# A hybrid decoder trunk on one core: half words joined after five weight units instead of two, and one block of queries turned by TensorE

## The chip, the cores and the metric

The kernel runs on 1 core of one Trainium2 chip. The metric is the device time of one execution in microseconds. A core has TensorE (PE in the profile; PEld is its weight load), VectorE (DVE), ScalarE (ACT), GpSimd (POOL) and SyncE (SP), and 16 DMA engines that all issuing queues share.

## The reference

Two post-norm layers on 256 tokens of width 2048. Each layer has a mixer of two head groups and a SwiGLU block:

```
def _hybrid_mixer(x, positions, w_in, ...):
    qa, ka, va, qi, wi, ki, cq, ckv, kr = split(x @ w_in)
    qa, ka = _rope(qa, rot 32), _rope(ka, rot 32)            # group A: 8 heads of 128
    qi, ki = _rope(qi, rot 16), _rope(ki, rot 16)            # indexer: 16 heads of 64
    score = sum over heads of relu(qi . ki) * wi, causal     # picks the top 64 keys of a query
    out_a = softmax(qa . ka over the picked keys) @ va
    q_b = _rms_norm(cq, g_cq) @ w_uq                         # group B (MLA): 8 heads
    q_nope, q_pe = q_b[..., :128], _rope(q_b[..., 128:], rot 64)
    kv = _rms_norm(ckv, g_ckv) @ w_ukv                       # k_nope, v_b
    out_b = causal softmax of (q_nope . k_nope + q_pe . _rope(kr)) @ v_b
    return concat(out_a, out_b) @ w_o

x = _layer_norm(ALPHA * x + mixer(x));  x = _layer_norm(ALPHA * x + swiglu(x))
```

All inputs and outputs are float32.

## The kernel before

**Weight units.** All tokens stay on the chip and the weights stream past them. A weight unit is 2 x 128 rows by 512 columns: one 512 KB load (`raw`) from SyncE's queue, split into two parts of reduced precision, `wh` by ACT (L427) and `wl` by DVE (L428), and then twelve matmuls on TensorE (two token tiles, two row blocks, three products: L391 to L393). There are five buffers of `wh` and of `wl` in this stage (`UNITS`), and four of `raw`. A projection chunk of 512 columns (`in_chunk`, `dsa_qk`, `dsa_v`) is 8 units.

**Tasks and ticks.** What has to be done with a projection's result (rope, turning, attention) is written as Python generators. `spawn` starts one; `tick()` stands after each weight unit and counts `units_gone`; a generator that yields `n` goes on `n` units later; `behind(...)` yields one unit at a time until other tasks are done, and `finish(...)` runs tasks out. So the position of a step in the program is counted in weight units.

**Order.** The program order that results is a priority. When the program is built, the tile framework sets each engine's own order: among the instructions that it reckons ready it takes the earliest in program order, so one whose operands or buffers it reckons not ready is passed by later ones (`tc.high_priority` raises a few by hand). On the chip each engine then runs its list strictly in order and waits where an operand is late.

**The attention stage of a layer** in program order, with its weight units: QI0 (8 units, first half of the indexer queries), TA (8), QI1 (8, second half), TB (8, the low-rank inputs `cq`, `ckv`), KA0 (8, four heads' keys of group A), then 2 units for the rope part of the MLA queries (`w_uq[2]`), `mla_half(0)` (4 ticks: queries `qn` twice, keys `kn`, values `vb`), QA0 (8), VA0 (8), `mla_half(1)`, KA1, QA1, VA1, and the output projection. The tasks:

- `heads_T` (L605 to L630) ropes a projection of 512 columns on DVE (L284 to L288) and turns it, 128x128 by 128x128, so that features stand on partitions. It does so with the DMA: ACT parts each 32-bit word into its half words (`pl`, L619), a transposing DMA that ACT issues turns the half words (L622), and ACT joins them again into `dst` (L627). It is used for QI0, QI1, KA0, QA0, KA1, QA1 and the rope queries: 7 blocks of two token tiles in each layer. Its yields: 1 after the rope, 1 after each token tile's parting and DMA, then 2 more, then a join and 1 for each tile.
- `indexer` (L702) waits behind TA's, QI0's and QI1's tasks, makes the scores in six steps of two units each (matmuls L714, ACT's relu L719, DVE's weighted sum L724) and then picks the top keys on DVE, 8 a unit (L731, L732).
- `mla_attend(hp)` (L773) handles two heads: it waits `wait` units and behind the rope queries' task (for the first two pairs), puts the logits into one PSUM pair of banks that all `att()` users share (L788 for the plain part, L792 for the rope part), and goes through `attend` (L562): DVE reads the logits (L571), softmax on DVE and ACT (L555 to L560), three transposes on TensorE into a bank of `trp()` (L424, two banks in turn), ACT copies (`pr`, L582), and one unit later the product with the values (L589).
- `dsa_attend(hp)` (L812) does the same for group A, behind the indexer and the tasks of its keys and queries.

The other work of this stage that shares the queues: `presums` (L833) loads weight blocks of the SwiGLU from POOL's queue, adds them on DVE (L852 to L856) and stores the sums. The small working tiles `ra`, `rb`, `hd`, `pl`, `lg`, `pr`, `rel` all come out of ten buffers of 2 KB a partition (`t2`).

Of the kernel before, what the change touches and what calls it, by code (L numbers as in the profile page):

```python
# [28 lines left out]
AF = mybir.ActivationFunctionType  # L29
# [4 lines left out]
P = 128  # L34
D = 2048
S = 256
NT = S // P
# [26 lines left out]
BYK = 3  # L64
SOON = 200
FIRSTD = 2
T2, T2MORE = 4, 6
ALLFROM, SETSFROM, EARLY = 3, 4, 0

# [16 lines left out]
def hybrid_trunk(ctx: ExitStack, tc: tile.TileContext, x, xt_in, pos, w_in, g_cq, g_ckv, w_uq,  # L86
                 w_ukv, w_o, ln1_g, ln1_b, ln1_T, w_gu, w_down, ln2_g, ln2_b, ln2_T, out):
    nc = tc.nc
# [11 lines left out]
    def t8(shape, dt, s):  # L100
        return sb.tile(shape, dt, name=nm(s), tag="a8", bufs=10)
# [17 lines left out]
    def t4(shape, dt, s):  # L119
        return pt(shape, dt, s, "a4", 8)  # L120

    def t2(shape, s, dt=F32):
        if phase["name"] == "att":
            phase["t2"] = phase.get("t2", 0) + 1
            if phase["t2"] * T2MORE % (T2 + T2MORE) < T2MORE:
                return pt(shape, dt, s, "t2", T2MORE)
        return sb.tile(shape, dt, name=nm(s), tag="t2", bufs=T2)
# [10 lines left out]
    def in_turn(s, first, n):  # L138
        turns[s] = turns.get(s, -1) + 1
        return bank(first + turns[s] % n, s)  # L140
# [4 lines left out]
    def trp():  # L145
        return in_turn("tr", 4, 2)
# [71 lines left out]
    sinM = const.tile([P, NT, 2, 32], F32, name="sinM")  # L218
# [57 lines left out]
    def rope(dst, src, nh, hd, rot, cos, sin):  # L276

        half = rot // 2
        s3 = src.rearrange("p (h d) -> p h d", d=hd)
        d3 = dst.rearrange("p (h d) -> p h d", d=hd)  # L280
        a = t2([P, nh, 2, half], "ra")
        b = t2([P, nh, 2, half], "rb")
        for j in range(2):
            nc.vector.tensor_tensor(a[:, :, j, :], s3[:, :, j * half:(j + 1) * half],  # L284
                                    cos.unsqueeze(1).to_broadcast([P, nh, half]), op=ALU.mult)
            nc.vector.tensor_tensor(b[:, :, j, :], s3[:, :, (1 - j) * half:(2 - j) * half],
                                    sin[:, j, :].unsqueeze(1).to_broadcast([P, nh, half]), op=ALU.mult)
        nc.vector.tensor_tensor(d3[:, :, 0:rot], a.rearrange("p h j k -> p h (j k)"),  # L288
                                b.rearrange("p h j k -> p h (j k)"), op=ALU.add)
# [19 lines left out]
    def spawn(gen):  # L309
        task = [0, gen]  # L310
        tasks.append(task)
        step(task)
        return task
# [5 lines left out]
    def finish(*ends):  # L319
        while any(e in tasks for e in ends):  # L320
            for task in list(tasks):
                if any(e in tasks for e in ends):
                    step(task)
# [53 lines left out]
    def proj(units, lhs, n, before=None, split_t=None, banks=None):  # L377

        o = [bank(i, "acc") for i in banks] if banks else [acc() for _ in range(NT)]
        loaded = []
        last = len(units) - 1

        def go(t, u):
            (wh, wl), ks = loaded[u], units[u][1]
            for j, k in enumerate(ks):
                h, l = lhs(t, k)
                a, b = wh[:, j, :n], wl[:, j, :n]
                first, final = u == 0 and j == 0, u == last and j == len(ks) - 1  # L390
                mm(o[t][:, :n], h, a, start=first, stop=False)  # L391
                mm(o[t][:, :n], h, b, start=False, stop=False)  # L392
                mm(o[t][:, :n], l, a, start=False, stop=final)  # L393

        def go_by_k(u):

            (wh, wl), ks = loaded[u], units[u][1]
            for j, k in enumerate(ks):
                xs = [lhs(t, k) for t in range(NT)]
                for i, w in ((0, wh), (1, wh), (0, wl)):  # L400
                    for t in range(NT):
                        mm(o[t][:, :n], xs[t][i], w[:, j, :n], start=u == i == j == 0 and w is wh, stop=False)

        for u, (src, ks) in enumerate(units):
            if before is not None:
                before(u)
            early = before is not None and u < BYK
            loaded.append(load_unit(src, src.shape[-1], KU if early else 1))
            if early:
                go_by_k(u)  # L410
            else:
                for t in range(1 if split_t else NT):
                    go(t, u)
            tick()
        if split_t:
            split_t()
            for u in range(len(units)):
                go(1, u)
                tick()
        return o  # L420

    def transpose4(srcs, psum):
        for i, s in enumerate(srcs):
            nc.tensor.transpose(psum[:, i * P:(i + 1) * P], s, ident)  # L424
# [169 lines left out]
    def layer(l, xT, norms, last):  # L594
        xk = xlhs(xT)

        def in_chunk(b, before=None, split_t=None):
            n = IN_BLOCKS[b][1]
            return proj([(w_in[b][l, u], range(u * KU, (u + 1) * KU)) for u in range(NKT // KU)], xk, n,
                        before, split_t)  # L600
# [1 line left out]
        cosI = [cosA[:, t, 0::2] for t in range(NT)]  # L602
        sinI = [sinA[:, t, :, 0::2] for t in range(NT)]

        def heads_T(o, nh, hd, rot, cos, sin, dst):  # L605


            ss = []
            for t in range(NT):
                s = t2([P, C], "hd")  # L610
                if rot < hd:
                    nc.scalar.activation(s, o[t], AF.Copy)
                rope(s, o[t], nh, hd, rot, cos[t], sin[t])
                ss.append(s)
            yield 1
            turned = []
            for s in ss:
                h16 = t2([P, 2 * C], "pl", U16)
                nc.scalar.activation(h16.rearrange("p (h c) -> p h c", h=2),  # L619
                                     s.bitcast(U16).rearrange("p (c h) -> p h c", h=2), AF.Copy)  # L620
                v = s.bitcast(U16).rearrange("p (k t) -> p k t", t=P)
                nc.scalar.dma_start_transpose(v, h16)  # L622
                turned.append(v)
                yield 1
            yield 2
            for t in range(NT):
                nc.scalar.activation(  # L627
                    dst[:, :, t * P:(t + 1) * P].bitcast(U16).rearrange("p k (t h) -> p h k t", h=2),
                    turned[t].rearrange("p (h k) t -> p h k t", h=2), AF.Copy)
                yield 1  # L630
# [131 lines left out]
        def mla_half(hf):  # L762
            qn = t4([P, 4, S], F32, "qn")
            kn = t4([P, 4, S], F32, "kn")
            vb = t4([P, NT, C], F32, "vb")
            nope_T(qn, [w_uq[hf][l, u] for u in range(2)], QL // P, cqT)
            nope_T(kn, [w_ukv[hf][l, 0]], KVL // P, ckvT)
            o = proj([(w_ukv[2 + hf][l, 0], range(2))], ckk, C)
            for t in range(NT):
                nc.scalar.activation(vb[:, t, :], o[t], AF.Copy)  # L770
            return qn, kn, vb
# [100 lines left out]
        if l == 0:  # L872
            turn("att")
            warm_up(18)
            o = in_chunk(QI0, load_xT)
            make_masks()
            rope_tables()
        else:
            o = in_chunk(QI0, None, lambda: finish(*norms))
# [9 lines left out]
        qpT = t4([P, M_HEADS // 2, S], F32, "qpT")  # L889
        bias = [pt([P, P * (t + 1)], F32, f"selb{t}") for t in range(NT)]  # L890
        o = in_chunk(TA)
        aff(1)
        p_ta = spawn(ta_post(o))
        aff(2)
        o = in_chunk(QI1)
        p_qi1 = spawn(heads_T(o, 8, I_DIM, I_ROT, cosI, sinI, qiT[1]))
        aff(3)
        p_ix = spawn(indexer())
        o = in_chunk(TB)
        p_tb = spawn(tb_post(o))  # L900
        if l == 0:
# [3 lines left out]
        finish(p_tb)  # L905
        o = proj([(w_uq[2][l, u], range(u * KU, (u + 1) * KU)) for u in range(QL // P // KU)], cqk, C)
        p_qp = spawn(heads_T(o, M_HEADS, M_ROPE, M_ROPE, [cosM[:, t] for t in range(NT)],
                             [sinM[:, t] for t in range(NT)], qpT))
        m = mla_half(0)
        b = [spawn(mla_attend(0, m, 1, p_qp)), spawn(mla_attend(1, m, 4, p_qp))]  # L910
        qa, p_qa = dsa_qk(QA0)
# [17 lines left out]
        for c in range(D // C):  # L929
            o = proj([(w_o[l, c, k // KU], range(k, k + KU)) for k in first], olhs, C)  # L930
# [271 lines left out]
        def spawn_hidden(fc, g, u):  # L1202
            hT = t8([P, 2, 4, S], F32R, "hT")
            held.append((fc, hT, spawn(hidden(g, u, hT, 3, 2 if fc + 1 < FIRSTD else 4))))

# [4 lines left out]
        def down_half(fc):  # L1210

            down(held[:2], (2, 3) if fc % 2 else (0, 1), ((2, 3), (0, 1)), first_operands if fc == ALLFROM else None)
            if fc % 2:
                del held[:2]
# [13 lines left out]
        for fc in range(1, NFC):  # L1228
            order = ORDER.get(fc, "SSQS")
            if fc >= FIRSTD:  # L1230
                down_half(fc)
                finish_hidden()
            g, u = gate_up(fc, [({"N": "plain", "S": "wino", "Q": "made", "T": "two"}[k], v) for k, v in zip(order, UNIT[order])],
                           finish_hidden if fc < FIRSTD else None)
            if fc < FIRSTD:
                for c in range(2, D // C):
# [18 lines left out]
    for l in range(DEPTH):  # L1255
        xT, norms = layer(l, xT, norms, l == DEPTH - 1)
# [51 lines left out]
```

## Time and profile before

| | us |
|---|---|
| median of 3 runs | 2172.12 |
| lowest, highest run | 2170.91, 2173.5 |
| the profiled execution | 2171.01 |
| its span, first to last instruction | 2169.2 |

The profile shows one execution, on the one core. The granted TensorE clock is 0.996 of full over the span. In the page, a group's line gives the source line, engine and operation, output and inputs by the program's names, the count, busy time and mean duration, and the idle time of its engine just before with what ended it. In a timeline, a line gives start, duration, engine, source line and operation, and in brackets the idle time before it and what released it; ACTq is ACT's queue when it issues a DMA, during which ACT starts nothing else. The attention stage is roughly 0 to 335 us in layer 0 and 1106 to 1420 us in layer 1.

### The profile page before, as it was taken

How to read it: one execution, taken by the hardware profiler on the slowest of the kernel's cores; microseconds unless marked ns; L12 is line 12 of the kernel's file. 1: busy time of each engine (PE TensorE's matmuls, PEld its weight loads, DVE VectorE, ACT ScalarE, POOL GpSimd, SP SyncE). 2: the span in 40 equal slices, each digit the busy share in tenths (PEclk: the TensorE clock that was granted, in tenths of full speed). 3: DMA queues.
4: the chain of work that ended last, by engine and by line, in shares of the span. 5: the costliest groups of instructions: out<-in, count | busy, mean ns of one | idle time of the engine just before them, and what ended most of it. 6: DMA issues, size and time to landing. Idle time of an engine off the chain costs nothing.

```text
span 2169.2 us, 28289 instructions
## 1 busy us (share of the span) xinstructions
PE 2125.2 (98%) x9830; PEld 1757.5 (81%) x9830; DVE 1859.4 (86%) x2359; ACT 1358.0 (63%) x1730; POOL 330.7 (15%) x527
## 2 busy tenths in 40 slices
PE   8999999999999999999999899999999999999998
PEld 7877888888878888888878788888888888888886
DVE  6596776899999999999855977768999999999997
ACT  6565664666666667766655565547666766666673
POOL 1112220021111101110012213200211111101111
PEclk9999999999999999999999999999999999999999
DMA  8878888578988889988678889895888988889884
GB/s 257 267 220 312 284 320 313 189 210 272 252 255 284 276 285 288 278 270 260 213 161 241 274 277 313 296 331 175 214 266 257 267 276 279 284 276 298 271 302 122
DMA packets 192336, 568.69 MB, mean 262 GB/s; under 512 B 47824, under 2 KB 48128, under 8 KB 191552
## 3 DMA queue, kind: packets, MB, share of 16 engines
q1 hardware_dynamic: 110736, 398.38, 51.5%
q0 software_dynamic: 51600, 160.77, 29.1%
q10 hardware_dynamic: 29856, 7.74, 2.6%
q8 instruction: 77, 1.26, 0.2%
q14 instruction: 67, 0.55, 0.1%
HBM read 506.51 MB, written 31.46 MB: 248 GB/s over the span
## 4 chain that ended last, share of the span: by engine, by line
PE 74%; DVE 9%; DMA 7%; issue 6%; ACT 3%; POOL 1%; ACTq 0%; SPq 0%; DVEq 0%; POOLq 0%
PE acc L1175 7%; PE acc L1176 7%; PE acc L1174 7%; PE acc L392 6%; PE gu_p L1060 6%; PE gu_p L1057 6%; PE gu_p L1059 6%; PE acc L393 6%; PE acc L391 6%; DVE wl L428 4%; PE gu_c L1059 3%; PE gu_c L1060 3%; PE gu_c L1057 3%; DMA hd<-pl 2%; DMA raw<-in_w_in_dram 2%
## 5 line engine op out<-in xcount | busy, mean ns | idle before, releaser
L428 DVE TENSOR_TENSOR wl<-raw,wh 128x1024 fp32r<-128x1024 f32 (+2 forms) x925 | 1088.2, 1211 | 206.6 <-ACT wh L427 203.9
L427 ACT ACTIVATE wh<-raw 128x1024 fp32r<-128x1024 f32 (+2 forms) x925 | 946.2, 1049 | 499.3 <-PE acc L1176 93.5
L391 PE MATMUL acc<-wh,xhl 128*128 128x512 f32 (+1 forms) x756 | 297.5, 394 | 4.4 <-ACT wh L427 4.4
L392 PE MATMUL acc<-wl,xhl 128*128 128x512 f32 (+1 forms) x756 | 293.9, 389 | 3.1 <-DVE wl L428 3.0
L393 PE MATMUL acc<-wh,xhl 128*128 128x512 f32 (+1 forms) x756 | 293.5, 389 | 0.0
L1175 PE MATMUL acc<-wl,hT 128*128 128x512 f32 x640 | 249.5, 390 | 1.0 <-DVE wl L428 0.8
L1174 PE MATMUL acc<-wh,hT 128*128 128x512 f32 x640 | 250.3, 392 | 0.0
L1176 PE MATMUL acc<-wh,hT 128*128 128x512 f32 x640 | 249.4, 390 | 0.0
L391 PEld LDWEIGHTS acc<-wh,xhl 128*128 128x128 f32 x756 | 142.6, 189 | 36.5 <-ACT wh L427 7.5
L392 PEld LDWEIGHTS acc<-wl,xhl 128*128 128x128 f32 x756 | 142.9, 189 | 31.3 <-DVE wl L428 5.7
L393 PEld LDWEIGHTS acc<-wh,xhl 128*128 128x128 f32 x756 | 142.7, 189 | 27.3
L1175 PEld LDWEIGHTS acc<-wl,hT 128*128 128x128 f32 x640 | 120.2, 188 | 26.8 <-DVE wl L428 2.5
L1176 PEld LDWEIGHTS acc<-wh,hT 128*128 128x128 f32 x640 | 120.1, 188 | 25.1
L1174 PEld LDWEIGHTS acc<-wh,hT 128*128 128x128 f32 x640 | 120.2, 188 | 24.3
L1183 POOL DMA_DIRECT2D x<-d x80 | 67.9, 849 | 427.4 <-ACT d L1182 425.9
L1059 PE MATMUL gu_c<-wl,xhl 128*128 128x512 f32 x336 | 131.1, 390 | 0.2
L1060 PE MATMUL gu_c<-wh,xhl 128*128 128x512 f32 x336 | 130.7, 389 | 0.0
L1057 PE MATMUL gu_c<-wh,xhl 128*128 128x512 f32 x336 | 130.7, 389 | 0.0
L1182 ACT ACTIVATE d<-acc 128x512 f32<-128x512 f32 x80 | 47.7, 596 | 76.0 <-PE acc L1176 76.0
L1059 PE MATMUL gu_p<-wl,many 128*128 128x512 f32 x240 | 93.5, 390 | 0.0
L1057 PE MATMUL gu_p<-wh,many 128*128 128x512 f32 x240 | 93.5, 389 | 0.0
L1060 PE MATMUL gu_p<-wh,many 128*128 128x512 f32 x240 | 93.4, 389 | 0.0
(306 smaller groups left out, 3867.6 us busy)
## 6 DMA issues: line engine op xcount, KB each, us to landing
raw<-in_w_gate_dram SPq DMA_DIRECT2D x176, 512.0 KB, 5.5
raw<-in_w_down_dram SPq DMA_DIRECT2D x176, 512.0 KB, 7.8
raw<-in_w_in_dram SPq DMA_DIRECT2D x144, 512.0 KB, 5.4
sum<-in_w_up_dram POOLq DMA_DIRECT2D x124, 512.0 KB, 7.4
raw<-in_w_up_dram SPq DMA_DIRECT2D x100, 512.0 KB, 5.7
raw<-in_w_o_dram SPq DMA_DIRECT2D x64, 512.0 KB, 6.5
q<-q POOLq DMA_DIRECT2D x56, 512.0 KB, 4.7
raw<-q SPq DMA_DIRECT2D x56, 512.0 KB, 5.8
```

Of the source, the lines that this page charges most:

```text
L391: mm(o[t][:, :n], h, a, start=first, stop=False)
L392: mm(o[t][:, :n], h, b, start=False, stop=False)
L393: mm(o[t][:, :n], l, a, start=False, stop=final)
L427: nc.scalar.activation(hi, src, AF.Copy)
L428: nc.vector.tensor_tensor(lo, src, f(hi), op=ALU.subtract)
L1057: mm(o[name], h, a, start=name not in begun, stop=False)
L1059: mm(o[name], h, b, start=False, stop=False)
L1060: mm(o[name], l, a, start=False, stop=end)
L1174: mm(o[c][t], h, wh[:, j, :], start=begin, stop=False)
L1175: mm(o[c][t], h, wl[:, j, :], start=False, stop=False)
L1176: mm(o[c][t], lo, wh[:, j, :], start=False, stop=end)
L1183: nc.gpsimd.dma_start(xt[t][:, c * C:(c + 1) * C], d, accum_op=ALU.add)
```

## The change

The fixed `yield 2` between the last transposing DMA of a block and its first join becomes `yield LAND` with `LAND = 5`. It holds for all blocks that the DMA turns. And the rope queries' block no longer goes by the DMA: with `soon` set, `heads_T` yields 3 units after the rope, then turns each token tile with four TensorE transposes into a PSUM bank and copies the bank into `dst` with one ACT instruction.

```
+LAND = 5
...
-        def heads_T(o, nh, hd, rot, cos, sin, dst):
+        def heads_T(o, nh, hd, rot, cos, sin, dst, soon=False):
...
                 rope(s, o[t], nh, hd, rot, cos[t], sin[t])
                 ss.append(s)
+            if soon:
+                yield 3
+                for t in range(NT):
+                    tp = trp()
+                    transpose4([ss[t][:, j * P:(j + 1) * P] for j in range(4)], tp)
+                    nc.scalar.activation(dst[:, :, t * P:(t + 1) * P], tp.rearrange("p (k t) -> p k t", k=4), AF.Copy)
+                return
             yield 1
             turned = []
...
                 turned.append(v)
                 yield 1
-            yield 2
+            yield LAND
             for t in range(NT):
                 nc.scalar.activation(
...
         p_qp = spawn(heads_T(o, M_HEADS, M_ROPE, M_ROPE, [cosM[:, t] for t in range(NT)],
-                             [sinM[:, t] for t in range(NT)], qpT))
+                             [sinM[:, t] for t in range(NT)], qpT, True))
```

## The prediction

> **What bounds the kernel now.** I read the page first, then the list of waits for TensorE alone, then the granted clock in short stretches, and only then the ACT and DVE timelines around those places.
>
> ```profile
> span 2169.2 us, 28289 instructions
> PE 2125.2 (98%) x9830; PEld 1757.5 (81%) x9830; DVE 1859.4 (86%) x2359; ACT 1358.0 (63%) x1730; POOL 330.7 (15%) x527
> 1281.46 1.06 ACT L427 ACTIVATE wh<-raw 128x1024 fp32r<-128x1024 f32 x1 [1.61 <-PE acc L393]
> 1284.18 1.06 ACT L427 ACTIVATE wh<-raw 128x1024 fp32r<-128x1024 f32 x1 [1.66 <-PE acc L393]
> ```
>
> TensorE is busy 98% of the span. In undisturbed stretches ACT waits for PE before each weight split, and two such splits start 1284.18 - 1281.46 = 2.72 us apart: that is one weight unit, and it is the unit in which the lags of this kernel count. So only what stops TensorE matters. The change touches the attention stage of the two layers; these are TensorE's waits there (seven windows; layer 0, then layer 1; columns: waiting line, what it waited for, us in total, times, longest):
>
> ```profile
> PE acc L391 <- ACT wh L427: 2.4, 2, 1.8
> PE acc L392 <- DVE wl L428: 1.5, 2, 0.8
> PE acc L753 <- DVE rb L286: 1.7, 2, 1.1
> PE acc L391 <- ACT wh L427: 1.7, 1, 1.7
> PE tr L424 <- ACT pr L582: 3.8, 1, 3.8
> ...
> PE acc L392 <- DVE wl L428: 1.5, 2, 0.8
> PE acc L391 <- ACT wh L427: 0.3, 1, 0.3
> PE acc L753 <- DVE rb L286: 2.3, 2, 2.1
> PE att L788 <- DVE lg L571: 3.7, 1, 3.7
> ```
>
> The first two (3.9 us, window 40 to 56) and the later L392 and L391 pair (1.8 us, 1105 to 1131) lie beside the joins of the first indexer block, QI0. The L753 rows are the second half of `mla_half(0)` waiting for DVE to finish reading the rope queries' PSUM banks. The 1.7 (window 151 to 168), the 3.8 (176 to 190) and the 3.7 (1244 to 1253) lie in the first two pairs of MLA heads. Four of these waits have a second price:
>
> ```profile
> 157.00:161.00 4.00, 4.00 (x13) 3.13 (x13) 4.00 (x4) 2.35 (x4) 1.12 (x2) 0.63 0.79 244
> 184.00:187.00 3.00, 3.00 (x8) 2.31 (x7) 2.76 (x7) 0.99 (x3) 0.58 (x1) 0.50 0.86 321
> 1225.00:1228.20 3.20, 3.02 (x15) 2.85 (x14) 3.02 (x7) 2.30 (x5) 0.34 (x1) 0.50 0.78 47
> 1248.40:1252.50 4.10, 4.10 (x17) 2.70 (x18) 4.03 (x21) 2.81 (x9) 0.00 (x0) 0.58 1.01 392
> ```
>
> The third number from the right is the granted clock (the columns before it are the stretch and PE, PEld, DVE, ACT, POOL busy). Right behind the waits of 1.7, 3.8, 2.3 and 3.7 us it is 0.63, 0.50, 0.50 and 0.58. Time lost: 0.37 x 4.0 = 1.5, 0.5 x 3.0 = 1.5, 0.5 x 3.2 = 1.6 and 0.42 x 4.1 = 1.7 us.
>
> **The lag of five units.** A unit's weight split goes to ACT as early as one of five `wh` buffers allows, so ACT runs some five units ahead of TensorE; a join, by contrast, has a place in program order only. Whether the lag sets the moment of a join can be read from the joins themselves (the two rows on L627's waits and landings, and one block in ACT's timeline):
>
> ```profile
>   DMA hd<-pl: 44.4, 18
> DMA to landing us min/median/max: 3.3/5.7/13.3
> 82.87 1.06 ACT L619 ACTIVATE pl<-hd 128x1024 uint16<-128x1024 uint16 x1 [0.56 <-ACT wh L427]
> 83.84 0.86 ACT L427 ACTIVATE wh<-raw 128x800 fp32r<-128x800 f32 x1
> 83.96 1.50 ACTq L622 DMA_TRANSPOSE hd<-pl  x1
> 88.09 1.38 ACT L627 ACTIVATE qiT<-hd 128x1024 uint16<-128x1024 uint16 x1 [3.40 <-DMA hd<-pl]
> ```
>
> The program puts three units (8.2 us at 2.72) between a block's second transposing DMA and its first join, and the median landing takes 5.7 us. Yet 18 of the 28 joins had to wait for the DMA, and here only one split (83.84) stands between the second `pl` and the join. The joins therefore stand where the scheduler reckoned the data there, and the run-ahead has used up the lag of two. Raising it to five moves the program place by three splits, just about the run-ahead. I take it that the joins of QI0 stay where they are (gain 0); the other end is that both of them pass behind the splits and all 3.9 + 1.8 = 5.7 us go.
>
> What the lag does move is the program behind `behind(...)`, since TensorE, always busy, keeps program order. Counting yields from the layer's start, QI1's block is done at unit 34, not 31, so the indexer's six steps go to TensorE at 34 to 44, not 31 to 41. QA0's block is done at 64, not 61: the first DSA pair's logits move from 63 to 64 and stand two units before the next pair's (66), not three; the same for the last two pairs (92 and 94). Both pairs share one PSUM tile, which DVE must have read:
>
> ```profile
> 306.37 1.48 PE L823 MATMUL att<-qk,qk 128*128 128x128 f32 x8
> 310.55 1.01 DVE L571 SCALAR_TENSOR_TENSOR lg<-att,selb 128x256 f32<-128x256 f32 x2
> 133.36 0.48 DVE L724 SCALAR_TENSOR_TENSOR score<-rel,wi,score 128x256 f32<-128x256 f32 x1
> ```
>
> Here DVE had read it 311.56 - 307.85 = 3.7 us after the logits; two units give 5.4 us, so this costs nothing, and it would cost if DVE came 1.7 us later. The indexer's last two steps now fall at 42 and 44, beside the rope of the rope queries at 42; before, it was the last one at 41. One more step is 4 x 0.48 = 1.9 us of DVE in each layer in front of L753's wait, while two steps fewer lie in the backlog before it. Bounds: +3.8 us, and -(1.7 + 2.3 + 1.6) = -5.6 us if the L753 waits go; I take 0, because these waits stand beside one indexer step before and after.
>
> **The rope queries by TensorE.** Removed per layer: two `pl` copies, two transposing DMAs, two joins, all on ACT's queue, and two t2 buffers. Added: eight transposes on TensorE and two copies on ACT.
>
> ```profile
> 143.92 1.04 ACT L619 ACTIVATE pl<-hd 128x1024 uint16<-128x1024 uint16 x1
> 144.99 1.25 ACTq L622 DMA_TRANSPOSE hd<-pl  x1
> 146.67 0.39 PE L391 MATMUL acc<-wh,ckvT 128*128 128x512 f32 x1
> 146.79 1.06 ACT L619 ACTIVATE pl<-hd 128x1024 uint16<-128x1024 uint16 x1 [1.34 <-DVE hd L288]
> 153.04 1.34 ACT L627 ACTIVATE qpT<-hd 128x1024 uint16<-128x1024 uint16 x1
> 154.24 1.04 ACT L427 ACTIVATE wh<-raw 128x1024 fp32r<-128x1024 f32 x1
> 143.44 0.58 ACT L756 ACTIVATE qn<-acc 128x512 f32<-128x512 f32 x1
> 177.38 0.82 PE L424 MATMUL tr<-ident,lg 128*128 128x128 f32 x6
> ```
>
> Step A, layer 0. The split at 154.24 is the one TensorE waited 1.7 us for. ACT loses 2 x (1.04 + 1.25) + 1.34 = 5.9 us ahead of it and gets two copies out of PSUM of the size of the `qn` one, 2 x 0.58 = 1.2. The split comes up to 4.7 us earlier, more than the wait: 1.7 and the slow clock's 1.5 go, 3.2 us.
>
> Step D, layer 1. Today the rope block is done at unit 49, so the first pair's logits (49) and the second's (50) stand one unit apart on the one PSUM tile; that is the wait of 3.7. With the block turned at 45 the first pair goes at 47, the second stays at 50: three units, 8.2 us, against the 3.7 us that DVE needed above. 3.7 + 1.7 = 5.4 us go.
>
> Step B, layer 0. The two pairs' transposes both stand at unit 53 today, on two PSUM banks, and the second ones wait for the first ones' copies:
>
> ```profile
> 181.45 1.06 ACT L427 ACTIVATE wh<-raw 128x1024 fp32r<-128x1024 f32 x1 [1.09 <-DMA raw<-in_w_in_dram]
> 182.42 0.85 ACT L582 ACTIVATE pr<-tr 128x384 f32<-128x384 f32 x2
> ```
>
> They will stand at 51 and 53. But the copies `pr` at 182.42 were late because ACT stood in line behind a split that waited for its weights, and the attention product at 52 needs those copies too. Of 3.8 + 1.5 = 5.3 us I take half, 2.7, with 0 and 5.3 as ends.
>
> Added on TensorE: 0.82 / 6 = 0.14 us each, 16 in all, 2.2 us, hidden by nothing. Waiting for their operand is left at 0: in layer 0 the second block's rope released its `pl` at 146.79, and `kn` had ended when the value projection began at 146.67, so the operand is there as it is wanted. The wait would hold all of TensorE, and it is the third rival below.
>
> Sum: -3.2 - 5.4 - 2.7 + 2.2 = -9.1 us on the profiled execution's 2171.0 (span 2169.2): 2161.9. The median of the runs is 2172.1, 1.1 above it, so the forecast is 2163.0.
>
> [...]
>
> **Rivals.** First, the lag does move QI0's joins. For it: five is the number of `wh` buffers, so the joins' program place falls behind the run-ahead. Against it: 18 of 28 joins were put ahead of data that their lag would have covered. Time: 2163.0 - 5.7 = 2157.3.
>
> Second, the MLA waits move instead of going. The heads are now turned two units apart, and the first pair's product stands one unit (2.72 us) behind its transposes; if `pr` is late there in both layers, as at 182.42, layer 0 keeps its 5.3 us and layer 1 gets the same. -3.2 - 5.4 + 2.2 + 5.3 = -1.1: 2171.0. For it: ACT's queue still waits for weights. Against it: layer 1 shows no such wait today.
>
> Third, slower: the new transposes stop TensorE. They stand at unit 45 in its queue, ahead of the value projection and of QA0, and they need DVE's last rope step.
>
> ```profile
> 1224.83 0.41 DVE L286 TENSOR_TENSOR rb<-acc,sinM 128x256 f32<-128x256 f32 x1
> 1231.39 0.69 DVE L288 TENSOR_TENSOR hd<-ra,rb 128x512 f32<-128x512 f32 x1
> 1228.08 0.50 PE L391 MATMUL acc<-wh,ckvT 128*128 128x512 f32 x1
> 1229.58 1.38 ACT L627 ACTIVATE qk<-hd 128x1024 uint16<-128x1024 uint16 x1
> ```
>
> In layer 1 that step ended at 1232.08, 4.0 us after `kn` had ended and the value projection had begun (1228.08). It started right behind a join of KA0's block (1229.58 + 1.38 = 1230.96), whose end frees a t2 buffer, and with the longer lag that join is ranked three units later. With the indexer's shift the same in layer 0, each layer pays 4.0 + 1.6 = 5.6: 11.2 + 2.2 - 3.2 - 5.4 = +4.8 us, 2176.9. It decides from 3.2 us a layer, clock included. Against it: the two `pl` buffers that competed with this step are gone, and its inputs were ready at 1225.24, some 6 us before.
>
> [...]
>
> **How the numbers follow.** Forecast 0.42 (2163.0), joins moved as well 0.26 (2157.3), waits moved 0.18 (2171.0), transposes stop TensorE 0.14 (2176.9). A measurement of this kernel can tell about 0.2%, 4.3 us, from no change: faster is below 2167.8, slower above 2176.4. Faster: the first two and a little of the third, 0.70. Slower: most of the fourth, 0.12. Same: 0.18. Range: below, the first rival with the other half of B and half of the L753 waits, 2157.3 - 2.6 - 2.8 = 2151.9; above, the second rival and 2 us for bounds taken at 0, 2173. Outside lie the fourth case and little else.
>
> **What would show it.** Right: no TensorE wait at L391 behind `kn`'s copies in layer 0, none at L788 in layer 1, three units between the first two MLA logits, two slow-clock stretches fewer, 24 transposing DMAs and 16 more L424 matmuls; QI0's joins still behind the same splits and still waiting. First rival: QI0's joins behind the next two splits, no TensorE wait at 40 to 56. Second: waits at L589 on `pr`. Third: waits at L424 on `hd`. The forecast is wrong if the waits of A or D remain, or if new waits over 3 us stand in a place that it does not name.

## The result, and the profile after

| | before | after |
|---|---|---|
| median of the runs, us | 2172.81 (4 runs, 2170.91 to 2174.3) | 2153.36 (4 runs, 2149.63 to 2156.64) |
| ratio, 95% interval | 1 | 0.991 (0.9891 to 0.993) |
| the profiled execution, us | 2171.01 | 2152.09 |

The changed kernel takes 19.5 us less. The forecast was 2163.0, 9.1 less: the sign was right, the time lies inside the range near its lower end, and the gain was about twice as large as forecast. Line numbers in the changed kernel are one higher up to the rope in `heads_T` and 8 higher behind the new branch there: the split is now L428 and L429, the projection's matmuls L392 to L394, `transpose4` L425, the relu L727, qn's and kn's matmuls L761 to L763, the joins L635.

The page of the changed kernel, and what the working tile `hd` waited for:

```profile
PE 2121.6 (99%) x9846; PEld 1760.4 (82%) x9846; DVE 1858.3 (86%) x2359; ACT 1350.5 (63%) x1726; POOL 330.0 (15%) x527
```

```profile
  DMA hd<-pl: 30.8, 15
DMA to landing us min/median/max: 3.4/5.6/11.3
```

There are 16 matmuls more, and 15 of 24 joins still wait for the transposing DMA, 30.8 us in all (18 of 28 and 44.4 us before). TensorE's waits in the attention stage, from QI0's joins to the first two MLA pairs, in eight windows that are wider than those of the prediction (layer 0 first, then layer 1; both layers have a row of 3.5):

```profile
PE tr L425 <- ACT kpT L653: 0.7, 1, 0.7
PE att L722 <- ACT rel L727: 0.4, 1, 0.4
PE acc L761 <- DVE ra L285: 3.5, 1, 3.5
PE tr L425 <- DVE hd L289: 1.6, 1, 1.6
...
PE tr L425 <- ACT cq L660: 1.7, 1, 1.7
PE acc L393 <- DVE wl L429: 0.7, 1, 0.7
PE acc L761 <- DVE ra L285: 3.5, 1, 3.5
PE tr L590 <- ACT pr L583: 0.4, 1, 0.4
```

The rows of 2.4, 1.5, 1.7 and 3.8 of layer 0 and the 3.7 of layer 1 are gone, and so are the rows of 1.7 and 2.3 for the rope queries' banks (L753 of the kernel before). Two more waits of the kernel before, at the indexer's scores, stand in no window of the prediction; they have come down to 0.4 in each layer (layer 0, then layer 1, in the kernel before):

```profile
PE att L714 <- ACT rel L719: 2.8, 1, 2.8
PE att L714 <- ACT rel L719: 2.2, 1, 2.2
```

One large row is new and stands in both layers: the first matmul of `qn` (L761) waits 3.5 us for a rope (L285). It has a second price, in the clock (third number from the right):

```profile
129.60:132.00 2.40, 2.38 (x11) 2.40 (x12) 2.36 (x9) 1.06 (x1) 0.00 (x0) 0.50 0.18 68
132.00:136.60 4.60, 4.60 (x29) 4.60 (x29) 3.15 (x7) 2.97 (x4) 0.00 (x0) 0.67 1.02 184
1200.90:1204.00 3.10, 3.10 (x15) 3.10 (x16) 2.25 (x8) 1.52 (x2) 0.00 (x0) 0.50 0.34 81
1204.00:1207.70 3.70, 3.70 (x22) 3.70 (x22) 3.07 (x7) 2.52 (x4) 0.00 (x0) 0.61 0.92 207
```

Lost behind the wait: 0.50 x 2.4 + 0.33 x 4.6 = 2.7 us in layer 0, 0.50 x 3.1 + 0.39 x 3.7 = 3.0 us in layer 1. The new wait so costs 6.2 and 6.5 us in this profile. The timeline shows what it is:

```profile
118.22 1.14 PE L722 MATMUL att<-kiT,qiT 64*128 64x256 f32 x8 [0.42 <-ACT rel L727]
119.94 1.09 ACT L727 ACTIVATE rel<-att 128x512 f32<-128x512 f32 x2
120.90 1.11 ACT L613 ACTIVATE hd<-acc 128x512 f32<-128x512 f32 x2
125.69 0.29 DVE L739 MAX8 m<-score 128x8 f32<-128x128 f32 x1
127.02 0.48 DVE L732 SCALAR_TENSOR_TENSOR score<-rel,wi,score 128x256 f32<-128x256 f32 x1
128.07 0.22 DVE L285 TENSOR_TENSOR ra<-acc,cosA 128x64 f32<-128x64 f32 x1
129.39 0.22 DVE L285 TENSOR_TENSOR ra<-acc,cosA 128x64 f32<-128x64 f32 x1
129.62 0.55 PE L761 MATMUL acc<-cqT,wh 128*128 128x256 f32 x1 [3.53 <-DVE ra L285]
```

KA0's keys lie in a PSUM bank that `qn` is to use next. ACT had copied them by 122.01 (120.90 + 1.11), but DVE's rope reads the bank too, and it starts at 128.07 only. DVE was busy all the time between: with two weight splits, five rounds of picking the first token tile's top keys (the last one at 125.69) and two of the scores from 127.02 on. Those scores belong to the indexer's step at unit 40, whose matmuls ran at 118.22 and whose relus ended at 121.03 (119.94 + 1.09). The matmul of `qn` starts as the rope's read at 129.39 ends (129.39 + 0.22 = 129.61), which the profile names as its releaser.

### The profile page after: what moved, and what is told of

It is laid out like the page before. It is cut to its first block, busy times and chain, and to the rows that moved or that the text cites. A ratio compares the mean times of both kernels' runs of the same rounds, so it can differ in the third digit from the quotient of the medians.

```text
span 2150.3 us, 28301 instructions
## 1 busy us (share of the span) xinstructions
PE 2121.6 (99%) x9846; PEld 1760.4 (82%) x9846; DVE 1858.3 (86%) x2359; ACT 1350.5 (63%) x1726; POOL 330.0 (15%) x527
## 5 line engine op out<-in xcount | busy, mean ns | idle before, releaser
L429 DVE TENSOR_TENSOR wl<-raw,wh 128x1024 fp32r<-128x1024 f32 (+2 forms) x925 | 1090.0, 1213 | 202.5 <-ACT wh L428 200.0
L428 ACT ACTIVATE wh<-raw 128x1024 fp32r<-128x1024 f32 (+2 forms) x925 | 946.9, 1050 | 499.3 <-PE acc L1184 93.4
L392 PE MATMUL acc<-wh,xhl 128*128 128x512 f32 (+1 forms) x756 | 297.1, 394 | 0.0
L394 PE MATMUL acc<-wh,xhl 128*128 128x512 f32 (+1 forms) x756 | 292.5, 387 | 0.0
L392 PEld LDWEIGHTS acc<-wh,xhl 128*128 128x128 f32 x756 | 142.1, 188 | 29.4 <-issue 2.6
L394 PEld LDWEIGHTS acc<-wh,xhl 128*128 128x128 f32 x756 | 142.0, 188 | 27.3
```

The lines of the kernel that those rows point to most:

```text
L428: nc.scalar.activation(hi, src, AF.Copy)
L429: nc.vector.tensor_tensor(lo, src, f(hi), op=ALU.subtract)
```

## Experiments

My theory after seeing the traces: the two halves of the change act apart. TensorE's turning gives the forecast gain. The lag has two effects that the prediction put at nothing: it moves QI0's joins (gain), and through QI1's block it starts the indexer three units later, which takes waits from the scores and makes the new wait (about even). The rivals: the lag does nothing of weight; the lag carries the gain; or QI0's joins gained in layer 0 only because the load of x, the layer's input, was issued at another moment.

| kernel | median, us | ratio to before (95%) |
|---|---|---|
| the change, timed again | 2156.01 | 0.9916 (0.9899 to 0.9934) |
| lag of five alone | 2178.87 | 1.0036 (1.0022 to 1.0049) |
| lag alone, rope queries two | 2170.99 | 0.9995 (0.9978 to 1.0011) |
| turning alone | 2156.07 | 0.9933 (0.9908 to 0.9958) |
| turning alone, again | 2150.94 | 0.9902 (0.9882 to 0.9923) |
| turning, indexer 3 units later | 2161.3 | 0.996 (0.9945 to 0.9975) |
| turning, lag five for QI0 only | 2148.19 | 0.9894 (0.9875 to 0.9912) |
| the change, lag two for QI1 | 2147.21 | 0.988 (0.9864 to 0.9897) |
| the same, again | 2149.91 | 0.9903 (0.9883 to 0.9922) |
| the change, rope from the copy | 2166.26 | 0.9975 (0.9955 to 0.9995) |
| before, load of x later | 2171.97 | 1.0002 (0.9987 to 1.0016) |
| change, lag two for QI1, AV later | 2155.28 | 0.9922 (0.9905 to 0.994) |

Where a kernel was timed in two groups I weight the two ratios by their intervals: the change 0.9913 (plus or minus 0.0013), turning alone 0.9914 (0.0016).

**Turning alone, and lag alone.** The edits:

```
LAND = 2                                   # turning alone
```
```
- ... qpT, True))                          # lag alone
+ ... qpT))
```

> The rope queries turned by TensorE, with the lag of two kept. The prediction's sum was made for just this: 2163 us (9.1 us less), the three waits of the rope queries gone, QI0's joins and the indexer as before. If the lag is what carries the gain instead: 2168 to 2173. No wait of qn's first matmul for KA0's rope in either theory, because the indexer starts where it did.

> The turning alone once more, beside the next two: 2150 to 2158 us. Its first six times lay from 2149 to 2163, so its ratio is to be known better before the lag's share is read from it.

> The lag of five alone; the rope queries keep their transposing DMAs. My theory, that the two halves of the change act apart: the lag gains at QI0's joins, 6.8 us in layer 0 and 2.2 in layer 1 as the changed kernel showed, loses about 6.9 us in each layer to the wait of qn's first matmul for KA0's rope, and gains back about 11 where the indexer's waits (layer 0 at 110 to 122, layer 1 at 1187 to 1200) go: some 2160 to 2166 us. The rope queries' waits of the kernel before (after the kn copies in layer 0, between the first MLA logits in layer 1) stay. The rival of the prediction, that the lag moves nothing of weight: 2171 to 2174.

> The changed kernel itself, timed beside the others of this group: 2151 to 2156 us if the first time holds. The turning alone gave 0.9933 of the kernel before; if the lag of five adds nothing to it, the changed kernel's ratio lies within 0.991 to 0.995, and if the lag adds the 6.8 us that QI0's joins seemed to gain in layer 0, at 0.990 or below.

Measured: turning alone is as good as the whole change (0.9914 and 0.9913), and better than the 2163 that the prediction's sum gives for it; the lag alone is slower than before. The lag is then worth nothing on top of the turning (0.000, plus or minus 0.002), and my figure for the lag alone, 2160 to 2166, was wrong by some 15 us. TensorE's waits with the turning alone (its second run; layer 0, then layer 1):

```profile
PE acc L392 <- ACT wh L428: 2.1, 1, 2.1
PE acc L393 <- DVE wl L429: 1.5, 2, 0.8
PE att L722 <- ACT rel L727: 2.9, 1, 2.9
PE acc L761 <- DVE rb L287: 0.3, 1, 0.3
PE tr L590 <- ACT pr L583: 1.5, 1, 1.5
...
PE att L722 <- ACT rel L727: 2.0, 1, 2.0
PE tr L590 <- ACT pr L583: 2.0, 1, 2.0
```

QI0's joins (2.1 and 1.5; in its first run 0.3 and 0.8) and the scores (2.9, 2.0) are waited for as in the kernel before; the wait of 3.5 for KA0's rope is absent; the MLA waits of 1.7, 3.8 and 3.7 are gone, with 1.5 and 2.0 for `pr` in their place. With the lag alone (layer 0 row first):

```profile
PE att L796 <- DVE lg L572: 9.2, 1, 9.2
...
PE acc L392 <- ACT wh L428: 5.8, 1, 5.8
PE acc L392 <- ACT wh L428: 8.5, 1, 8.5
PE att L796 <- DVE lg L572: 4.3, 1, 4.3
```

Two things stand out in its trace. The rope queries' block, still turned by the DMA, is done three units later, so that both first MLA pairs, which wait behind it, start at unit 52: the second pair's logits wait 9.2 and 4.3 us for DVE to read the first pair's (L572). And in layer 1 two weight splits are late by 5.8 and 8.5 us behind joins whose transposing DMAs landed after 17.6 and 18.9 us. In these places the DMA engines showed a busy share of one and more and moved little (the same view as above; the last two numbers are the DMA share and GB/s):

```profile
1110.00:1119.00 9.00, 9.00 (x41) 7.44 (x41) 4.86 (x6) 1.70 (x2) 3.48 (x4) 1.00 1.23 107
1119.00:1127.00 8.00, 4.82 (x22) 3.65 (x20) 0.00 (x0) 1.37 (x1) 0.57 (x1) 1.00 1.63 68
1170.00:1182.00 12.00, 6.41 (x36) 6.06 (x34) 0.42 (x1) 0.00 (x0) 1.75 (x4) 0.93 1.12 157
```

In the changed kernel the place that answers to the last row (1154 to 1166) moved 374 GB/s.

**The lag alone, without the pairs at one unit.**

```
- ... qpT))
+ ... qpT, False, 2))                      # land = 2 for the rope queries, 5 elsewhere
```

> The lag of five for all blocks but the rope queries, which keep their transposing DMAs and the lag of two, so that the first two MLA pairs start at units 49 and 50 as before and not both at 52. If the lag alone was slower because both pairs then start at one unit: their waits of 9.4 us in layer 0 and 4.5 in layer 1 go, those of the kernel before (1.8 and 4.0 in layer 0, 3.8 in layer 1) come back, and the time is 3 to 6 us less than the lag alone, 2172 to 2176. If it was slower because of the transposes that landed after 18 us in layer 1 (weight splits late by 6.0 and 8.6 us): these stay, and 2177 to 2181.

```profile
PE att L800 <- ACT qpT L635: 4.8, 1, 4.8
...
PE acc L392 <- ACT wh L428: 4.5, 1, 4.5
PE acc L392 <- ACT wh L428: 8.5, 1, 8.5
```

Both theories hold for a part, and the time, 2171.0, is a little below both. The pairs' waits of 9.2 and 4.3 go (a wait of 4.8 for the joined rope queries and one of 1.4 come), and 7.9 us with them; the late splits of layer 1 stay at 4.5 and 8.5. So the lag without the turning gains nothing even when the pairs keep their distance. Why the transfers of layer 1 are so slow in both these kernels, and in none where TensorE turns the rope queries, no run tells.

**QI0's joins.** Two kernels: the kernel before with the load of x held back, and the turning with the lag of five at QI0's block only.

```
     def load_x():
+        not_until_now(*xt)                # behind TB's last split
```
```
-LAND = 5
+LAND = 2
...
+        p_qi0 = spawn(heads_T(o, 8, I_DIM, I_ROT, cosI, sinI, qiT[0], False, 5))
```

> The kernel before with the load of x (two of 1 MB, layer 0) held back until TB's last weights are split; lag and rope queries as before, and QI0's joins stand behind the same splits. If QI0's joins in layer 0 waited because the load of x was issued between their two transposing DMAs: the transposes land in about 4 to 6 us instead of 7.0 and 10.4, TensorE's waits at 40 to 56 go, and the time is 4 to 7 us less (2166 to 2169). If the lag itself is what helped there: transposes as slow as before and 2171 to 2174.

> The rope queries turned by TensorE, the lag of five for QI0's block alone, two for all others. If what the lag gives is that QI0's joins stand one weight split later, behind transposes whose landing varies from run to run: 4 to 9 us less than the turning alone, 2146 to 2152, like the kernel with the lag of two for QI1 only (2147). If the lag at the key and query blocks gives it: no less than the turning alone, 2154 to 2158. Either way no wait of qn's first matmul for KA0's rope.

The ACT timeline with the turning alone (second run), and then in the changed kernel:

```profile
35.69 0.68 SPq L187 DMA_DIRECT2D x<-in_x_dram  x1
37.49 2.14 ACTq L630 DMA_TRANSPOSE hd<-pl  x1
41.95 1.37 ACT L635 ACTIVATE qiT<-hd 128x1024 uint16<-128x1024 uint16 x1 [3.54 <-DMA hd<-pl]
48.18 1.34 ACT L635 ACTIVATE qiT<-hd 128x1024 uint16<-128x1024 uint16 x1 [3.96 <-DMA hd<-pl]
```

```profile
37.74 1.25 ACTq L630 DMA_TRANSPOSE hd<-pl  x1
39.09 1.06 ACT L428 ACTIVATE wh<-raw 128x1024 fp32r<-128x1024 f32 x1 [0.44 <-PE acc L394]
40.32 0.42 SPq L187 DMA_DIRECT2D x<-in_x_dram  x1
40.46 2.58 ACT L635 ACTIVATE qiT<-hd 128x1024 uint16<-128x1024 uint16 x2 [0.30 <-DMA hd<-pl]
```

The lag of five lets one split (39.09) pass ahead of both joins; with the lag of two a split stood between them. With the lag the order on SP's queue changes too: x (1 MB) is loaded behind both transposing DMAs, not between them. The joins then wait 0.3 us in place of 3.54 and 3.96. In time, from the end of QI0's units to the end of TA's, against the kernel before: the lag of two gave 0 (before), -3.5 and +1.2 (turning alone, twice), -3.8 (indexer later); the lag of five gave -4.2 to -5.1 in eight profiles, -4.9 in the mean. The first group's mean is -1.5, so this place is some 3.4 us faster with the lag of five.

That the later join brings it is not shown. Holding back x with the lag of two gave -4.1 at the same place, with no lag at all; there the time came back at the scores, which waited 6.8 us, and the sum was no change. Sorted by x, the profiles part more cleanly than by the lag: with x behind both transposing DMAs all nine lie at -4.1 to -5.1, and with x between them five lie at -3.8 to +5.3. The two transposing DMAs landed after 3.5 to 6.9 us in the nine and after 5.1 to 15.0 us in the five. The +5.3 has the lag of five (the rope from the copy, below). So the place of x, which the lag happened to change, is the likelier cause; the lag of five with x held where it was has not been run on its own. The turning with lag five at QI0 alone fell in the expected 2146 to 2152; against the turning alone (0.9894 to 0.9914) the intervals overlap. In layer 1 no such gain is seen: 0, +1.5 (x held back), -2.9, -2.9 and +1.8 us with the lag of two, -1.2 to -2.9 with the lag of five where TensorE turns the rope queries, +6.6 and +5.2 where the DMA does.

**The indexer's start and the new wait.** Three kernels: the turning with the lag of two, but QI1's task ending three units later; the change with the lag of two at QI1 (timed twice); and the change with the rope reading ACT's copy, not the bank.

```
+            if tail:                      # heads_T's end; tail = 3 for QI1
+                yield tail
```
```
+        p_qi1 = spawn(heads_T(o, 8, I_DIM, I_ROT, cosI, sinI, qiT[1], False, 2))
```
```
-                rope(s, o[t], nh, hd, ...
+                rope(s, s if rot < hd else o[t], nh, hd, ...
```

> The rope queries turned by TensorE, joins with the lag of two everywhere, but QI1's task ends three units later, so that the indexer starts at unit 34 as in the changed kernel and not at 31. If the later indexer is the cause of both the waits of the scores that went and of the new wait of qn's first matmul for KA0's rope (3.5 us and the slow clock behind it in each layer): that wait appears here and not with the turning alone, the score waits of layer 0 (1.7 and 2.3 us) and of layer 1 (2.2 and 1.4) are gone, and the time is within 4 us of the turning alone, either way. If KA0's own joins with lag five made the new wait: no such wait here.

> The changed kernel with the lag of two for QI1's block alone, so that the indexer starts at unit 31 again; the lag is five for QI0 and the key and query blocks, and the rope queries are turned by TensorE. If the later indexer makes the wait of qn's first matmul and takes away the scores' waits: the one is gone, the others are back (about 3 us in layer 0, 2 in layer 1), and the time is that of the turning alone, 2153 to 2159. If the wait of qn's first matmul came from the lag of other blocks: it stays, and 2158 or more.

> The lag of two for QI1's block alone, once more, since its first four times rest on one group: if the lag of QI1 costs what the two traces showed (3.5 us and 2.7 to 3.0 us of slow clock in each layer, less some 5 us of score waits in layer 0 and 3 in layer 1), 4 to 8 us less than the changed kernel's 0.9913, a ratio of 0.988 to 0.990. If the first figure was chance: 0.991 or more.

> The changed kernel, but where a block is first copied out of its PSUM bank, the rope reads that copy and not the bank, so that the bank is free when ScalarE's copy is done. If qn's first matmul waited only because VectorE's rope of KA0 still read the bank behind the indexer's work: the wait of 3.5 us and the slow clock behind it (about 3.4 us) go in both layers, and the time is 7 to 14 us less than the changed kernel's, 2140 to 2147. If VectorE's backlog is the limit, the wait comes back at the next bank that VectorE must read (the rope queries' own, not copied): 2149 to 2154.

The change with the lag of two at QI1 (layer 0, then layer 1):

```profile
PE att L722 <- ACT rel L727: 2.5, 1, 2.5
PE acc L761 <- DVE rb L287: 0.3, 1, 0.3
PE tr L590 <- ACT pr L583: 1.5, 1, 1.5
...
PE att L722 <- ACT rel L727: 2.1, 1, 2.1
PE tr L590 <- ACT pr L583: 2.2, 1, 2.2
```

The wait for KA0's rope (3.2 to 3.5 us in each layer) stands in all five profiles in which the rope reads the bank and the indexer starts at unit 34 (the change twice, the lag alone, the lag with rope queries two, the turning with the indexer later), and in none of the eight in which it starts at 31. The scores' waits do the opposite. The indexer's start is so shown to be the cause of both. Its balance, from QI1's end to VA0's end, a stretch that holds all six steps of the indexer in either case: with the change the kernel is 5.1 us (layer 0) and 4.9 us (layer 1) ahead of the one before, with the turning alone 6.9 and 6.0: the later start loses 1.8 + 1.1 = 2.9 us (means of two profiles each). In the one profile of the turning with the later indexer the same stretches lose 5.0 us against the turning alone. Its time is 0.0046 or 10 us (plus or minus 5) behind the turning alone, more than the 4 us expected; another 4.7 us of it lie at QI0's joins in layer 1, ahead of the indexer.

By the times, the three kernels with the turning, lag five at QI0 and lag two at QI1 have 0.9891 (plus or minus 0.0010) together, the change 0.9913 (0.0013): 0.0022 or 4.8 us, plus or minus 3.6, which holds both figures. The kernel with the lag of two at QI1 came out below the expected 2153 to 2159 both times (2147 and 2150). These three are the best kernels of the study; keeping the lag of two at QI1 beats the change.

Freeing the bank earlier does not help:

```profile
PE acc L392 <- ACT wh L428: 7.0, 1, 7.0
...
PE att L722 <- ACT rel L727: 2.9, 2, 2.4
PE acc L761 <- DVE rb L287: 2.1, 1, 2.1
```

The wait of 3.5 goes, and in its place the scores' matmuls wait 2.9 us and `kn` 2.1 us for the rope queries' rope, in both layers (2.9 and 1.7 in layer 1). In this profile the limit is DVE's backlog, as the rival had it. The 7.0 is another matter: in this profile the second transposing DMA of QI0 landed after 15.0 us (the load of x was issued between the two again, at 36.20), which the lag of five does not cover either. It holds 10.2 us of the distance to the others with that lag (+5.3 from QI0's end to TA's, not -4.9), and the time is worse than both theories had it.

**The product with V one unit later.**

```
-        yield 1                           # in attend, ahead of the product; MLA pairs only
+        yield late
```

> The best so far (rope queries by TensorE, lag five but two for QI1's block) with the MLA pairs' product with V one unit later. There TensorE waited 1.7 us in layer 0 and 2.4 in layer 1 for the copies of the turned probabilities (pr). If those waits are simply early work: they go, 3 to 5 us less, 2142 to 2145. If ScalarE's queue is what sets them: they move behind the next split, 2146 to 2149.

This met neither expectation. The waits for `pr` in the first two pairs went, and the next transposes waited 1.2 and 1.8 us for the bank that the later product held (L425 behind the split of `oB`, L429). At 0.9922 it is slower than without (0.9891). Its profile gives back 5.5 us of its lead in layer 1 behind VA0, where the second two pairs stand; what stops TensorE there was not taken apart.

## Why the prediction was right in its sign and too small

- **Only what stops TensorE matters: held.** The differences looked at between the kernels show up as its waits and the slow clock behind them.
- **Steps A and D: right.** No wait behind `kn`'s copies in layer 0, none between the first two MLA logits in layer 1, and no slow clock there.
- **Step B: too small.** I took half of 5.3 us; the wait for `pr` at the second transposes went whole. With the turning alone the product then waits 1.5 us, in the changed kernel not at all in layer 0.
- **The L753 waits, taken as unchanged: mis-sized.** With the turning alone they fell from 1.7 to 0.3 us in layer 0 and from 2.3 to 1.5 in layer 1, and layer 1's slow clock of 1.6 behind them went; in the changed kernel they are gone.
- **The added transposes: 1.6 us, not 2.2.** Eight of them held TensorE for 0.79 us a layer:

```profile
145.68 1.03 PE L425 MATMUL tr<-ident,hd 128*128 128x128 f32 x8
146.47 0.48 PE L392 MATMUL acc<-wh,ckvT 128*128 128x512 f32 x1
```

These steps make the turning. From KA0's end to VA0's end it brought 8.6 and 3.9 us (means of two profiles), 12.5 where the sum had 9.1. By its times it brought 0.0086 of 2172, 18.7 us, plus or minus 3.5. Some 5 us more stand in layer 1 ahead of these steps (2.9 at QI0's joins, 2.0 between TB's and KA0's end). The 2.9 is missing in the kernel with the indexer later, which turns by TensorE too, so it may be chance; its cause stays open.

That the time fell inside the range is so in part luck: the range's lower end was made from QI0's joins, the other half of B and half of the L753 waits, and what the time holds beyond the sum is more of B, the L753 waits and these 5 us.

- **QI0's joins, taken as staying: the step failed.** The first of the two joins moved behind one more split in both layers. The place is 3.4 us faster in layer 0, with nothing to be seen in layer 1. The first rival was nearly right on the motion (it had two splits) and had 5.7 us for it; whether the motion or the place of x brought the 3.4 stays open, and the profiles speak for x.
- **The indexer's shift, taken as 0 with +3.8 as its upper bound: the step failed.** It costs 2.9 us by the profiles of the change (5.0 where it stands alone with the turning). This is a balance of terms that the sum did not have: the new wait costs 6.2 and 6.5 us, and against it went the scores' waits of 2.8 and 2.2 us, which the prediction's windows left out, and the rest of the L753 waits. I had weighed the steps at 42 and 44 against the rope of the rope queries alone; in DVE's order the scores of the step at unit 40 and the picks of the first token tile stood ahead of KA0's rope, whose bank `qn` needs. By the prediction's own test, a new wait of over 3 us in a place that it does not name, this part of the forecast was wrong.
- **The rivals.** The second (waits for `pr` at the product) came to 1.5 and 2.0 us with the turning alone (in its second run the clock was 0.61 and then 0.82 in the 6 us from 1240 on, 1.7 us lost), and to 0.4 in the change. The third came to 1.6 us in layer 0 (2.4 in the second timing's profile) and nothing in layer 1, below the 3.2 from which it decides. The DSA pairs two units apart cost nothing: TensorE's longest wait there is 0.3 us.
- **The parts were summed as if apart.** The lag's two failed steps nearly cancel (3.4 against 2.9). But the lag without the turning is worse than the kernel before by 0.0036, because it moves the rope queries' end to where both MLA pairs start together, and with it came the slow transfers of layer 1; the turning was worth 0.0086 with the lag of two, and 1.0036 - 0.9913 = 0.0123 with the lag of five.

## What to carry to other kernels

A lag in program order moves everything that waits behind the lagged task, not the lagged step alone: follow each dependent task to its new place, and count what it puts in front of every engine's next urgent read, PSUM banks above all. Give such a lag block by block; here it went with a gain where a DMA's landing varied (QI0) and cost where it started a long task later (QI1). When a lag seems to pay, look whether it also changed the order of transfers on another queue; here the time at QI0's joins followed that order more closely than the lag. A place that varies by 4 us between two profiles of one kernel needs several profiles before a gain there is believed.

## What the runs showed of the hardware

- **The clock.** Behind one wait of 3.5 us TensorE's granted clock was 0.50 until about 135.1 in layer 0 (the 0.67 over 4.6 us from 132.0 is the mean of 0.50 for 3.1 us and 1.00 for 1.5), almost as costly as the wait (2.7 and 3.0 us). In narrower stretches the clock is 1.00 from 126.10 to 128.24, inside the wait, 0.50 from there to 135.07, and 1.00 behind it. In the kernel before, it was 0.63 and 0.50 behind waits of 1.7 and 2.3 us, and 1.00 from 100 to 125, with the scores' wait of 2.8 us inside: the length of the wait alone does not sort these cases, and what does is not shown.
- **ACT's queue.** In the kernel before, the two copies `pr` at 182.42 started only as the split ahead of them ended, which had itself waited 1.09 us for its weights; the transposes that they copy had ended at 178.20 (177.38 + 0.82), 4.2 us earlier. An issue of a transposing DMA took 1.25 to 3.57 us there, and in 27 of 28 ACT started nothing before it ended (in the other, 0.05 us before). In the changed kernel so it was in 22 of 24; in one of the others it started an instruction 0.05 us before, and within the one at 1321.42 it started six of a softmax.
- **Transposing DMAs.** A transfer of 256 KB from SBUF to SBUF took 3.4 to 11.3 us (median 5.6) in the changed kernel, and up to 18.9 in the lag alone. Plain loads of 256 KB took from 3.8 (the norm's gain) to 7.4 us (its bias) in the median. No run isolates the late landings.
- **Rate.** The DMA engines showed a busy share of 1.2 to 1.6 while moving only 68 to 107 GB/s for 17 us (the lag alone, from 1110 on), against 261 in that kernel's mean. No run isolates the cause.
